# Keys projected first in differential attention, and a first layer whose loads and products come in another order

## The chip, the cores and the metric

The kernel runs on one core of one Trainium2 chip. The metric is the device time of one execution in microseconds. The kernel before takes 3145.52 us, the median of three runs (3144.89 to 3149.38). The profiled execution took 3149.2 us.

The engines are called PE (TensorE, matrix products), DVE (VectorE), ACT (ScalarE), POOL (GpSimd) and SP (SyncE, which here only issues transfers). SBUF is the on-chip memory that they work from, PSUM the one that PE's products are summed in.

## The reference: what is computed

Two transformer blocks run one after the other on 512 tokens of width 1024, in fp32. The first block has two layers and also carries 256 context tokens; the second has two layers of another kind (a gated convolution, dilated window attention, a gated recurrence), which the change leaves as they are.

Every layer normalizes its input and scales and shifts it by a modulation, which comes from a conditioning vector times a large matrix:

```
def _modulate(x, g, shift, scale):
    return _rms_norm(x, g) * (1 + scale) + shift
```

The first layer ("even") then projects tokens and context with `even_w_in`, and runs window attention and neighbourhood attention. The second ("odd") is differential attention with 8 heads. Each head has two query and two key halves of 64, values of 128, and keys and values from the 512 tokens and the 256 context tokens:

```
    q, k, v = _split_odd(hx @ w_in)
    cq, ck, cv = _split_odd(hc @ w_in)
...
    s = jnp.einsum('bqhmd,bkhmd->bhmqk', q, k).astype(jnp.float32) * d ** -0.5
    p = jax.nn.softmax(s, axis=-1)
    a = (p[:, :, 0] - lam * p[:, :, 1]).astype(v.dtype)
    o = jnp.einsum('bhqk,bkhe->bqhe', a, v)
```

Queries and keys of the tokens (not those of the context) are rotated by their position in a grid (rope). No query of the context is needed in this layer.

## The kernel before, in words

Activations lie in SBUF with the features on the 128 partitions, in 8 slices k, tokens along the free axis. To reach fp32 accuracy every operand is split into a high and a low part, and a product is made of three: `mm3` (L140 to L149) issues for each k high weight times high x (L147), high weight times low x (L148), and low weight times high x (L149). A projection of one chunk of 128 output features is 24 products with 512 columns for the tokens and 24 with 256 columns for the context. Its weight is loaded by `weight` (L132): SP issues the load into `wraw`, ACT casts the high part (L129), DVE subtracts the low part (L130). How many buffers `wraw` has is the first number in `b.weights(...)`.

The program is written as a sequence of operations on tiles, with a number of buffers for each tile name (`BUFS`, and `b.bufs.update`). A framework orders each engine's instructions by priorities and sets the semaphores; each engine then runs its own list in order. A transfer is issued by SP or, for the keys' copies, by POOL, in the order of that engine's list.

**The first layer's start, `start_even`.** SP issues the loads: the tokens hx, blocks `adan` of the modulation's matrix (8 of them are needed here, one per slice k), the small vectors, the weights of the first four chunks, the context hc, then constants (`rest()`). PE forms the mean of the squares of the tokens (L224, `xa<-sqx`) and of the context (`xa<-sqc`). Then for each k: `sums(k)` multiplies the conditioning vectors with block k of the matrix (L623), ACT copies the result (L715), `norm(k)` transposes it (L721), DVE adds it up, and `scaled` makes the normalized, modulated slice k of tokens and context, split in two (`axh`, `axl`, `ach`, `acl`). `project(k)` issues slice k of the projections (L733 to L735), two steps behind (`AHEAD`): before, of four chunks for the tokens and of two for the context. The sums lie in PSUM tiles `xa` and `ca`. The context of the last two chunks follows at the end by `mm3`. The four chunks are a key, a value and two query chunks; their chains end in the K, V and Q of the first attention: rope on DVE and POOL, casts on ACT (L302, L490), subtractions on DVE (L303, L491), transfers on POOL (L492, L493), and transposes of V on PE (L322).

**The odd attention, `layer_odd`.** For each head h and query block qb of 128 queries, `softmax` issues two sets of scores (four products each, `s<-K,Q`, L328 and L329: high and low part of the keys), a maximum on DVE (L862), an exponential on ACT (L864), and combines the two maps to `pr` (L865 to L868). `finish` does for the previous query block six transposes on PE (L876), copies on ACT (L877), and products with V (`o<-pT,V`, L879). In blocks 1, 2 and 3 `project(h + 1, part)` projects one part of the next head into the PSUM tile d, which has one buffer; `take` brings it out through a tile `raw`, which has two.

- Part 0, Q: only tokens. Rope (DVE shuffle L287, product with the cosine L288, POOL product with the sine L289, DVE sum L290), then two passes each on ACT (L302) and DVE (L303).
- Part 1, K: tokens and context. Rope, ACT copy of the context (L825), two ACT casts (L310), two DVE subtractions (L311), and four transfers K to K, issued by POOL (L313), that copy half of the partitions to the other half, so that high and low parts lie as the score products need them.
- Part 2, V: tokens and context, copies (L823, L825), six transposes on PE (L322), copies (L323).

The first head's three parts come from the end of the layer before (`first`), in the tile dd, and their order is the order of a list in the program.

Of the kernel before, what the change touches and what calls it, by code (L numbers as in the profile page):

```python
# [9 lines left out]
F32 = mybir.dt.float32  # L10
# [7 lines left out]
P = 128  # L18
D = 1024
KC = D // P  # L20
# [9 lines left out]


AHEAD = 2
BUFS = { "adan": 5, "xa": 4, "ca": 2, "sqx": 3, "sqc": 3, "nwx": 3, "nwc": 3, "adas": 1, "nw": 6, "nr0": 2, "nt": 2,
# [633 lines left out]
def start_even(b, st, mod, pset, chunks, hp, pp, rest):  # L667


    nc, io = b.nc, b.io  # L670
    raw = b.tile(hp, [P, KC, 2], F32, "craw")
    nc.sync.dma_start(raw, io["ccT"])
    nc.vector.memset(st, 0.0)
    nc.scalar.activation(st[:, :, :2], raw, AF.Silu)
    hx = b.tile(hp, [P, KC, T], F32, "hx")
    hc = b.tile(hp, [P, KC, TC], F32, "hc")

    def load(k):
        w = b.tile(hp, [P, KC, 256], F32, "adan")
        nc.sync.dma_start(w, io["ada_wa"][k])  # L680
        return w

    for i in range(0, KC, 2):
        nc.sync.dma_start(hx[:, i:i + 2], io["xT"][:, i:i + 2])
    aw = [load(0)]
    nc.sync.dma_start(b.vecs, io["vecs"])
    ws = [b.weight(io["even_w_in"][chunks[0]])]
    for i in range(0, KC, 4):
        nc.sync.dma_start(hc[:, i:i + 4], io["ctxT"][:, i:i + 4])
    ws.append(b.weight(io["even_w_in"][chunks[1]]))  # L690
    aw.append(load(1))
    ws += [b.weight(io["even_w_in"][ch]) for ch in chunks[2:]]
    aw += [load(k) for k in range(2, 5)]
    rest()
    gm = b.tile(hp, [P, KC], F32, "gm")
    nc.vector.tensor_scalar(gm, b.vec("norm1_g0"), -0.5, None, op0=ALU.mult)
    r = {}

    def rms(key, h, n):
        ms = b.mean(pp, b.squares(hp, n, lambda k: h[:, k], sq="sq" + key), n, tag="xa")  # L700
        r[key] = b.newton(hp, ms, n, key)

    rms("x", hx, T)
    ps = [{"x": b.tile(pp, [P, T], F32, "xa")} for _ in chunks]
    for p in ps[:2]:
        p["c"] = b.tile(pp, [P, TC], F32, "ca")
    parts = pset.all()
    mm = nc.tensor.matmul

    def sums(k):  # L710
        w = aw[k] if k < len(aw) else load(k)
        po = b.tile(pp, [P, 256], F32, "o")
        ada_mm(b, po, st, w)
        sb = b.tile(hp, [P, 256], F32, "adas")
        nc.scalar.copy(sb, po)  # L715
        return sb

    def norm(k, sb):
        pt = b.tile(pp, [P, T], F32, "t")
        for c in range(2):  # L720
            nc.tensor.transpose(pt[:, c * P:(c + 1) * P], sb[:, c * P:(c + 1) * P], b.ident)  # L721
        ada_sum(b, mod, k, 2, pt[:, :256])
        sc = b.tile(hp, [P, 2], F32, f"sc{k}")
        nc.vector.tensor_scalar(sc, mod[:, 8 + k], 1.0, gm[:, k:k + 1], op0=ALU.add, op1=ALU.mult)
        for v, (key, h) in enumerate((("x", hx), ("c", hc))):
            hi, lo = parts[key][k]
            b.scaled(hp, h[:, k], r[key], sc[:, v:v + 1], mod[:, k, v:v + 1], hi, lo, "nw" + key)

    def project(k):
        for (wh, wl), p in zip(ws, ps):  # L730
            for key in p:
                hi, lo = parts[key][k]
                mm(p[key], wh[:, k], hi, start=k == 0, stop=False)  # L733
                mm(p[key], wh[:, k], lo, start=False, stop=False)
                mm(p[key], wl[:, k], hi, start=False, stop=k == KC - 1)  # L735

    for k in range(KC + AHEAD):
        if k < KC:
            sb = sums(k)
        if k == 0:  # L740
            rms("c", hc, TC)
        if k >= AHEAD:
            project(k - AHEAD)
        if k < KC:
            norm(k, sb)
    for w, p in zip(ws[2:], ps[2:]):
        p["c"] = b.tile(pp, [P, TC], F32, "ca")
        b.mm3(p["c"], w, parts["c"])
    return parts, ps


def layer_even(b):
# [7 lines left out]
    with ExitStack() as ps0:  # L760
        pp = b.pool(ps0, "ps0", space=PSUM)
        with ExitStack() as s:
            b.weights(s, "w0", 2, 4)
            a, ps = start_even(b, st, mod, S0, first, b.pool(s, "h0"), pp, A.load)
        A.kp, A.pp = b.pool(att, "kp0"), pp
        for ch, p in zip(first, ps):
            A.take(ch, p)
# [31 lines left out]

def layer_odd(b, a, first, env):
    tc, nc, io = b.tc, b.nc, b.io
    side, other = env.ins.side, env.other
# [1 line left out]
    b.weights(wax, "wa1", 2, 2, side)  # L806
    yp = b.pool(yx, "Y1", side)
    at = b.pool(att, "at1", other)
    ws = [b.weight(io["odd_w_in"][8 * part + 1]) for part in range(2)]
    lam = diff_lambda(b, at)  # L810
    mean_v = b.tile(at, [P, P], F32, "mean_v")
    nc.vector.memset(mean_v, 1.0 / P)
# [5 lines left out]
    def take(part, ps, pp, tag):  # L818
        raw = b.tile(at, [P, TA], F32, "raw")
        if part < 2:  # L820
            b.rope(at, raw[:, :T], ps["x"])
        else:
            nc.scalar.copy(raw[:, :T], ps["x"])  # L823
        if part:
            nc.scalar.copy(raw[:, T:], ps["c"])  # L825
        if part == 0:
            q = b.tile(at, [P, 2, T], F32R, "Q1")
            b.qstack(q, raw, T)
            return (q,)
        if part == 1:  # L830
            k1, k2 = (b.tile(at, [P, 2, TA], F32R, t) for t in ("K1", "K2"))
            b.kstack(k1, k2, raw, TA)
            return k1, k2
        v = b.tile(at, [P, 6, P], F32, "V1")
        b.values(pp, v, raw, 6, tag)
        return (v,)

    def project(h, part):
        w = ws.pop(0) if ws else b.weight(io["odd_w_in"][8 * part + h])
        ps = {}  # L840
        for key, n in (("x", T), ("c", TC))[:1 if part == 0 else 2]:
            ps[key] = b.tile(pp, [P, T], F32, "d")[:, :n]
            b.mm3(ps[key], w, a[key])
        return take(part, ps, pp, "t")

    qkv = sum((take(part, ps, env.pp, "dd") for part, ps in enumerate(first)), ())
    env.pdx.close()
    pp = b.pool(ppx, "pp1", space=PSUM)

# [42 lines left out]
    Y = []  # L892
    before = None
    for h in range(8):
        after = ()
        po = b.tile(pp, [P, T], F32, "o")
        for qb in range(4):
            pr = softmax(qkv, qb)
            if before:
                finish(*before)  # L900
                if qb == 0:
                    Y.append(value(h - 1, before[1]))
            if qb and h < 7:
                after += project(h + 1, qb - 1)
            before = qkv[3], po, qb, pr
        qkv = after
    finish(*before)
    Y.append(value(7, po))

# [667 lines left out]
def program(tc, io):  # L1577
    with ExitStack() as left:
# [20 lines left out]
        nx, gx1 = b.modulation(modx, "norm1_g1", 0)  # L1599
        nc1, _ = b.modulation(modc, "norm1_g1", 0)  # L1600
        w = io["odd_w_in"]
        a, first = next_layer(b, env, rest, {"x": nx, "c": nc1}, streams, [(w[0], "x"), (w[8], "xc"), (w[16], "xc")])
        ops, slots = layer_odd(b, a, first, env)
        n2, g2 = b.modulation(modx, "norm2_g1", 1)
        mod = b.tile(b.cp, [P, 48], F32, "mod2_0")
# [69 lines left out]
```

## Time and profile before

| | |
|---|---|
| median of three runs | 3145.52 us |
| profiled execution | 3149.2 us |
| its span, first to last instruction | 3147.1 us |
| mean granted clock of PE | 0.989 of full speed |
| busy share of PE, DVE, ACT, POOL | 96%, 63%, 42%, 7% |

Times in the rows below are microseconds from the start of the span. A row of a timeline gives start, length, engine, line, operation, what is written and read, how many instructions are merged, and in brackets how long the engine stood idle before and what released it. A row of a stretch gives its length and, for each engine, its busy time and number of instructions, then PE's mean granted clock (1.00 is 2.4 GHz, 0.50 is 1.2 GHz), the share of the transfer engines' time, and GB/s. Products on PE overlap, so their lengths in a timeline add up to more than the time that passes.

### The profile page before, as it was taken

The numbers are of one execution on the slowest core, as the hardware profiler recorded it, in microseconds if no ns is written. First come the engines' busy times: TensorE is split into PE (matmuls) and PEld (weight loads), VectorE is DVE, ScalarE is ACT, GpSimd is POOL, SyncE is SP. The second block draws the span as 40 slices with busy tenths as digits, with TensorE's granted clock in tenths as the row PEclk, the third lists the DMA queues.
The fourth block names the chain that finished last, engine by engine and source line by source line (L and its number), as shares of the span: only waits on it lengthen the run. The fifth ranks groups of instructions, "written<-read, shape, count | busy, mean of one in ns | idle before, by whom it ended". The sixth has DMA issues, their size and how long they took to land.

```text
span 3147.1 us, 48350 instructions
## 1 busy us (share of the span) xinstructions
PE 3026.1 (96%) x19416; PEld 2484.1 (79%) x19416; DVE 1990.6 (63%) x3564; ACT 1310.1 (42%) x2290; POOL 217.7 (7%) x293
## 2 busy tenths in 40 slices
PE   7999999999998999899999999999999999999998
PEld 5776798888897877798888776698888777688887
DVE  6656475545436766676665885677865785674545
ACT  4656441222234555543223354652424354652422
POOL 0000100000011111000002111100001111100000
PEclk9999999999999999999999999999999999999999
DMA  6222423444312122246661232346662132323331
GB/s 241 91 88 91 141 81 121 128 122 127 120 34 66 45 60 54 92 139 189 189 192 41 75 88 82 121 126 190 193 186 76 55 88 81 121 88 95 100 89 52
DMA packets 100336, 342.78 MB, mean 109 GB/s; under 512 B 12176, under 2 KB 15888, under 8 KB 97040
## 3 DMA queue, kind: packets, MB, share of 16 engines
q1 hardware_dynamic: 93840, 325.53, 33.5%
q0 software_dynamic: 5120, 11.01, 1.8%
q8 instruction: 153, 2.51, 0.3%
q10 hardware_dynamic: 1152, 3.15, 0.3%
q14 instruction: 71, 0.58, 0.1%
HBM read 326.54 MB, written 2.10 MB: 104 GB/s over the span
## 4 chain that ended last, share of the span: by engine, by line
PE 80%; DVE 12%; ACT 3%; DMA 2%; issue 2%; POOL 1%; DVEq 0%; SPq 0%; POOLq 0%; ACTq 0%
PE dd L147 18%; PE dd L148 18%; PE dd L149 18%; PE d L147 3%; PE d L148 3%; PE d L149 3%; DMA K<-K 2%; PE o L597 1%; PE s L328 1%; DVE cy L1021 1%; DVE wlo L130 1%; PE s L329 1%; PE t L590 1%; PE o L1097 1%; ACT whi L129 1%
## 5 line engine op out<-in xcount | busy, mean ns | idle before, releaser
L147 PE MATMUL dd<-axh,whi 128*128 128x512 f32 (+1 forms) x2696 | 966.1, 360 | 6.1 <-ACT axh L243 5.9
L148 PE MATMUL dd<-axl,whi 128*128 128x512 f32 (+1 forms) x2696 | 967.0, 360 | 0.6 <-DVE axl L130 0.3
L149 PE MATMUL dd<-axh,wlo 128*128 128x512 f32 (+1 forms) x2696 | 964.7, 359 | 0.0
L129 ACT CAST whi<-wraw 128x1024 fp32r<-128x1024 f32 (+1 forms) x388 | 403.1, 1043 | 1027.1 <-PE dd L148 749.8
L130 DVE TENSOR_TENSOR wlo<-wraw,whi 128x1024 fp32r<-128x1024 f32 (+1 forms) x388 | 468.7, 1212 | 339.5 <-ACT whi L129 321.0
L147 PEld LDWEIGHTS dd<-axh,whi 128*128 128x128 f32 x2696 | 507.2, 189 | 85.1 <-ACT axh L243 7.9
L148 PEld LDWEIGHTS dd<-axl,whi 128*128 128x128 f32 x2696 | 508.3, 189 | 79.2 <-DVE axl L130 1.7
L149 PEld LDWEIGHTS dd<-axh,wlo 128*128 128x128 f32 x2696 | 508.1, 189 | 78.1
L181 DVE CUSTOM_DVE_ANT_0 adaj<-wraw,cond,vecs 128x1024 bf16<-128x1024 f32 x160 | 205.5, 1284 | 145.8 <-DMA wraw<-in_ada_w 87.8
L147 PE MATMUL d<-axh,whi 128*128 128x512 f32 x664 | 276.0, 416 | 6.6 <-ACT axh L129 4.7
L149 PE MATMUL d<-axh,wlo 128*128 128x512 f32 x664 | 272.3, 410 | 1.1 <-DVE wlo L130 1.1
L148 PE MATMUL d<-axl,whi 128*128 128x512 f32 x664 | 269.0, 405 | 0.7 <-DVE axl L130 0.7
L218 POOL TENSOR_TENSOR sq<-sq,sq 128x256 f32<-128x256 f32 x90 | 77.4, 871 | 1989.1 <-ACT sq L213 1871.1
L154 DVE SCALAR_TENSOR_TENSOR hx<-dd,mod,hx 128x512 f32<-128x512 f32 (+1 forms) x109 | 72.0, 661 | 173.8 <-PE dd L149 173.7
L148 PE MATMUL dd<-acl,whi 128*128 128x256 f32 x568 | 160.5, 283 | 0.0
L149 PE MATMUL dd<-ach,wlo 128*128 128x256 f32 x568 | 160.3, 282 | 0.0
L147 PE MATMUL dd<-ach,whi 128*128 128x256 f32 x568 | 160.2, 282 | 0.0
L147 PEld LDWEIGHTS d<-axh,whi 128*128 128x128 f32 x664 | 126.1, 190 | 37.0 <-ACT axh L129 6.1
L149 PEld LDWEIGHTS d<-axh,wlo 128*128 128x128 f32 x664 | 126.0, 190 | 32.1 <-issue 6.3
L148 PEld LDWEIGHTS d<-axl,whi 128*128 128x128 f32 x664 | 126.4, 190 | 27.7 <-issue 4.0
L328 PE MATMUL s<-K,Q 128*128 128x256 f32 (+1 forms) x336 | 116.1, 356 | 30.1 <-DMA K<-K 19.3
L329 PE MATMUL s<-K,Q 128*128 128x512 f32 (+1 forms) x336 | 108.8, 339 | 1.9 <-DMA K<-K 1.9
(384 smaller groups left out, 4470.4 us busy)
## 6 DMA issues: line engine op xcount, KB each, us to landing
wraw<-in_mlp_w SPq DMA_DIRECT2D x128, 512.0 KB, 3.6
wraw<-in_w_ada SPq DMA_DIRECT2D x96, 512.0 KB, 4.0
wraw<-in_w_up SPq DMA_DIRECT2D x88, 512.0 KB, 3.6
wraw<-in_w_in SPq DMA_DIRECT2D x56, 512.0 KB, 3.6
wraw<-in_ada_w SPq DMA_DIRECT2D x48, 512.0 KB, 3.6
adaw<-in_ada_wb SPq DMA_DIRECT2D x16, 1024.0 KB, 4.9
wraw<-in_w_down SPq DMA_DIRECT2D x32, 512.0 KB, 3.5
wraw<-in_odd_w_in SPq DMA_DIRECT2D x24, 512.0 KB, 3.7
```

What stands on the lines that cost most here:

```text
L129: self.nc.scalar.copy(hi, src)
L130: (e or self.nc.vector).tensor_tensor(lo, src, f32(hi), op=ALU.subtract)
L147: mm(ps, hi[:, k], xh[:, sl], start=first, stop=False)
L148: mm(ps, hi[:, k], xl[:, sl], start=False, stop=False)
L149: mm(ps, lo[:, k], xh[:, sl], start=False, stop=last)
L154: self.nc.vector.scalar_tensor_tensor(h, ps, gate[:, m:m + 1], h, op0=ALU.mult, op1=ALU.add)
L181: nc.vector.tensor_tensor_reduce(junk, raw, c, 1.0, self.vec(bias)[:, i:i + 1], ALU.mult, ALU.add, out[:, i:i + 1])
L218: e.tensor_tensor(acc, acc, s2, op=ALU.add)
L328: mm(ps, q[:, slot, toks], k1[:, keys], start=True, stop=False)
L329: mm(ps, q[:, slot, toks], k2[:, keys], start=False, stop=mask is None)
L590: last = nc.tensor.transpose(pt[:, o:o + P], pr[hd][:, i * P:(i + 1) * P], b.ident)
L597: mm = nc.tensor.matmul(po[64 * o:64 * o + 64], v, sbs[i][:, 2 * P * o:2 * P * (o + 1)], start=i == 0, stop=i == len(vts) - 1)
```

## The change

In the odd attention the three parts of the next head come in the order K, Q, V, set by `ORDER = (1, 0, 2)`, where they came as Q, K, V; the first head's parts and the weights loaded ahead follow the same order.

In `start_even` the loads are issued in another order: the second modulation block and the second weight now come before the context, and the constants (`rest()`) are issued at step 7. `wraw` has three buffers there, where it had two. In the loop only three chunks' tokens are projected (there were four); the context's mean is formed at step `LATE` = 2 (was 0), the context is scaled two steps behind the tokens and projected two steps further behind. The fourth chunk's tokens follow by `mm3` after the loop, then the context of the third and fourth. A PSUM tile `ca` has 512 columns and holds the context sums of two chunks: the first and third share one, the second and fourth the other.

The number of instructions is the same on every engine.

```diff
@@ start_even
-    aw = [load(0)]
+    aw, ws = [load(0)], []
     nc.sync.dma_start(b.vecs, io["vecs"])
-    ws = [b.weight(io["even_w_in"][chunks[0]])]
+    project = lambda i: ws.append(b.weight(io["even_w_in"][chunks[i]]))
+    more = lambda: aw.append(load(len(aw)))
+    project(0)
+    more()
+    project(1)
     for i in range(0, KC, 4):
         nc.sync.dma_start(hc[:, i:i + 4], io["ctxT"][:, i:i + 4])
-    ws.append(b.weight(io["even_w_in"][chunks[1]]))
-    aw.append(load(1))
-    ws += [b.weight(io["even_w_in"][ch]) for ch in chunks[2:]]
-    aw += [load(k) for k in range(2, 5)]
-    rest()
+    more()
+    project(2)
+    more()
+    more()
+    project(3)
...
-    ps = [{"x": b.tile(pp, [P, T], F32, "xa")} for _ in chunks]
-    for p in ps[:2]:
-        p["c"] = b.tile(pp, [P, TC], F32, "ca")
+    pc = [b.tile(pp, [P, T], F32, "ca") for _ in chunks[::2]]
+    ps = [{"x": b.tile(pp, [P, T], F32, "xa"), "c": pc[i % 2][:, i // 2 * TC:(i // 2 + 1) * TC]} for i in range(len(chunks))]
...
+        if k == KC - 1:
+            rest()
...
-        for v, (key, h) in enumerate((("x", hx), ("c", hc))):
-            hi, lo = parts[key][k]
-            b.scaled(hp, h[:, k], r[key], sc[:, v:v + 1], mod[:, k, v:v + 1], hi, lo, "nw" + key)
+        scs.append(sc)
+        scaled(k, 0, "x", hx)
+    def scaled(k, v, key, h):
+        hi, lo = parts[key][k]
+        b.scaled(hp, h[:, k], r[key], scs[k][:, v:v + 1], mod[:, k, v:v + 1], hi, lo, "nw" + key)
+    def project(k, key, n):
+        hi, lo = parts[key][k]
+        for (wh, wl), p in zip(ws[:n], ps):
...
     for k in range(KC + AHEAD):
         if k < KC:
             sb = sums(k)
-        if k == 0:
+        if k == LATE:
             rms("c", hc, TC)
         if k >= AHEAD:
-            project(k - AHEAD)
+            project(k - AHEAD, "x", 3)
+        if k >= AHEAD + LATE:
+            project(k - AHEAD - LATE, "c", 2)
         if k < KC:
             norm(k, sb)
+        if k >= LATE:
+            scaled(k - LATE, 1, "c", hc)
+    for k in range(KC + AHEAD - LATE, KC):
+        scaled(k, 1, "c", hc)
+    for k in range(KC - LATE, KC):
+        project(k, "c", 2)
+    b.mm3(ps[3]["x"], ws[3], parts["x"])
     for w, p in zip(ws[2:], ps[2:]):
-        p["c"] = b.tile(pp, [P, TC], F32, "ca")
         b.mm3(p["c"], w, parts["c"])
@@ layer_even
-            b.weights(s, "w0", 2, 4)
+            b.weights(s, "w0", 3, 4)
@@ layer_odd
+ORDER = (1, 0, 2)
-    ws = [b.weight(io["odd_w_in"][8 * part + 1]) for part in range(2)]
+    ws = [b.weight(io["odd_w_in"][8 * part + 1]) for part in ORDER[:2]]
...
-    qkv = sum((take(part, ps, env.pp, "dd") for part, ps in enumerate(first)), ())
+    join = lambda parts: parts[1] + parts[0] + parts[2]
+    qkv = join([take(part, ps, env.pp, "dd") for part, ps in zip(ORDER, first)])
...
-                after += project(h + 1, qb - 1)
+                after.append(project(h + 1, ORDER[qb - 1]))
...
-        qkv = after
+        qkv = join(after) if after else ()
@@ the program
-        a, first = next_layer(b, env, rest, {"x": nx, "c": nc1}, streams, [(w[0], "x"), (w[8], "xc"), (w[16], "xc")])
+        a, first = next_layer(b, env, rest, {"x": nx, "c": nc1}, streams, [(w[8], "xc"), (w[0], "x"), (w[16], "xc")])
```

How the change moves instructions is shown at two places. The first is PE at the end of a head (the one before the boundary at 1107.25 us of the trace). d is the projection of V, its tokens' last product first and its context's first and last; s are the next head's scores, t the transposes of V. Before:

```order
L149 MATMUL d_10633<-axh_1795_9015,wlo_10630 128x512
L328 MATMUL s_10703<-K_2101_10573,Q_2081_10461 128x512
L328 MATMUL s_10712<-K_2101_10573,Q_2081_10461 128x512
L147 MATMUL d_10658<-ach_1765_8985,whi_10629 128x256
...
L149 MATMUL d_10658<-ach_1779_8999,wlo_10630 128x256
L322 MATMUL t_10687<-ident_58,raw_10683 128x128 x4
L329 MATMUL s_10703<-K_2102_10574,Q_2081_10461 128x512
```

The same place on PE now:

```order
L150 MATMUL d_10631<-axh_1793_9013,wlo_10628 128x512
L329 MATMUL s_10701<-K_2080_10485,Q_2100_10576 128x512
L330 MATMUL s_10701<-K_2081_10486,Q_2100_10576 128x512
L329 MATMUL s_10701<-K_2080_10485,Q_2100_10576 128x256
L330 MATMUL s_10701<-K_2081_10486,Q_2100_10576 128x256
L148 MATMUL d_10656<-ach_1763_8983,whi_10627 128x256
...
L150 MATMUL d_10656<-ach_1777_8997,wlo_10628 128x256
L323 MATMUL t_10685<-ident_58,raw_10681 128x128 x4
L329 MATMUL s_10710<-K_2080_10485,Q_2100_10576 128x512
```

The first scores stand at the same place in both, behind the tokens' products of V; before, the first product of each set stood there, now the whole first set. On POOL, for the same head and the beginning of the next, before (rsh is the rotated half in rope, first Q's, then the keys'):

```order
L289 TENSOR_TENSOR rsh_10456<-rsh_10456,sin_132 128x512
L289 TENSOR_TENSOR rsh_10567<-rsh_10567,sin_132 128x512
L313 DMA K_2101_10573<-K_2101_10573 64x768 x2
L313 DMA K_2102_10574<-K_2102_10574 64x768 x2
L289 TENSOR_TENSOR rsh_10831<-rsh_10831,sin_132 128x512
```

And now (first the keys', then, behind their four transfers, Q's):

```order
L290 TENSOR_TENSOR rsh_10479<-rsh_10479,sin_477 128x512
L314 DMA K_2080_10485<-K_2080_10485 64x768
L314 DMA K_2081_10486<-K_2081_10486 64x768
L314 DMA K_2080_10485<-K_2080_10485 64x768
L314 DMA K_2081_10486<-K_2081_10486 64x768
L290 TENSOR_TENSOR rsh_10571<-rsh_10571,sin_477 128x512
```

The keys' product and transfers moved ahead of Q's product. The second place is the start of the program. SP's list before, from the small vectors on:

```order
L686 DMA vecs_66<-in_vecs 128x691
L135 DMA wraw_97<-in_even_w_in 128x1024
L689 DMA hc_89<-in_ctxT 128x1024 x2
L135 DMA wraw_105<-in_even_w_in 128x1024
L680 DMA adan_111<-in_ada_wa 128x2048
L135 DMA wraw_113<-in_even_w_in 128x1024
L135 DMA wraw_119<-in_even_w_in 128x1024
L680 DMA adan_125<-in_ada_wa 128x2048
```

And now:

```order
L687 DMA vecs_66<-in_vecs 128x691
L136 DMA wraw_97<-in_even_w_in 128x1024
L681 DMA adan_103<-in_ada_wa 128x2048
L136 DMA wraw_105<-in_even_w_in 128x1024
L694 DMA hc_89<-in_ctxT 128x1024 x2
L681 DMA adan_113<-in_ada_wa 128x2048
L136 DMA wraw_115<-in_even_w_in 128x1024
L681 DMA adan_121<-in_ada_wa 128x2048
```

The second block of the modulation (adan) and the second weight went ahead of the context, and the third block ahead of the third weight. PE's list at the start before (xa from sqx and sqc are the two means, o the modulation's sums, t their transposes, xa from axh the first projection):

```order
L224 MATMUL xa_173<-sqx_150,mean_d_64 128x512
L623 MATMUL o_219<-adan_94,cst_70 32x256 x8
L721 MATMUL t_261<-ident_58,adas_228 128x128 x2
L623 MATMUL o_276<-adan_111,cst_70 32x256 x5
L224 MATMUL xa_253<-sqc_230,mean_d_64 128x256
L623 MATMUL o_276<-adan_111,cst_70 32x256 x3
L733 MATMUL xa_181<-axh_60_187,whi_99 128x512
```

And now:

```order
L225 MATMUL xa_156<-sqx_133,mean_d_64 128x512
L624 MATMUL o_202<-adan_94,cst_70 32x256 x8
L727 MATMUL t_213<-ident_58,adas_211 128x128 x2
L624 MATMUL o_224<-adan_103,cst_70 32x256 x8
L727 MATMUL t_235<-ident_58,adas_233 128x128 x2
L624 MATMUL o_246<-adan_113,cst_70 32x256 x8
L225 MATMUL xa_280<-sqc_257,mean_d_64 128x256
L741 MATMUL xa_166<-axh_52_170,whi_99 128x512
```

The context's mean still stands ahead of the first projection; a pair of transposes and the third block's sums now do so too.

## Rows read from the trace of the kernel before

**Rows 1.** The page, busy time, share and instructions of each engine.
```profile
PE 3026.1 (96%) x19416; PEld 2484.1 (79%) x19416; DVE 1990.6 (63%) x3564; ACT 1310.1 (42%) x2290; POOL 217.7 (7%) x293
```

**Rows 2.** Waits of PE, 940 to 1330: total us, times, longest.
```profile
PE s L328 <- DMA K<-K: 19.3, 8, 3.3
...
PE t L876 <- DVE pr L868: 2.3, 6, 0.4
...
PE s L329 <- DMA K<-K: 1.9, 1, 1.9
```

**Rows 3.** Stretches of the odd attention: length, busy (count), clock, DMA.
```profile
1060.76:1104.52 43.76, 40.29 (x232) 34.15 (x232) 28.61 (x51) 23.03 (x42) 5.01 (x6) 0.96 0.23 56
...
1148.02:1189.75 41.73, 38.81 (x232) 32.67 (x232) 28.61 (x51) 23.02 (x42) 5.01 (x6) 1.00 0.23 56
...
1275.44:1312.00 36.56, 33.05 (x197) 27.68 (x197) 21.98 (x42) 20.29 (x40) 0.00 (x0) 0.95 0.25 76
```

**Rows 4.** Timeline of PE at a boundary between heads.
```profile
1107.25 0.47 PE L328 MATMUL s<-K,Q 128*128 128x512 f32 x1 [2.74 <-DMA K<-K]
```

**Rows 5.** Chain of waits at the same boundary: start, us, what.
```profile
1101.10 6.02 DMA K<-K
```

**Rows 6.** Timeline of DVE and POOL: the chain of Q.
```profile
1124.35 0.74 DVE L287 STREAM_SHUFFLE rsh<-d 128x512 f32<-128x512 f32 x1
...
1125.24 1.61 POOL L289 TENSOR_TENSOR rsh<-rsh,sin 128x512 f32<-128x512 f32 x1 [21.34 <-DVE rsh L287]
...
1129.82 1.39 DVE L303 SCALAR_TENSOR_TENSOR Q<-raw,Q 64x512 fp32r<-64x512 f32 x2
```

**Rows 7.** Stretches: V's x-products; two score sets and o.
```profile
1098.56:1104.13 5.57, 5.57 (x28) 4.59 (x26) 4.46 (x5) 2.21 (x3) 2.11 (x4) 1.00 0.45 103
1124.28:1127.10 2.82, 2.82 (x24) 2.64 (x22) 2.75 (x7) 1.73 (x4) 1.61 (x1) 1.00 0.00 0
```

**Rows 8.** Timeline of PE, ACT and POOL: the first head.
```profile
974.71 1.54 PE L322 MATMUL dd<-ident,raw 128*128 128x128 f32 x6 [6.87 <-ACT raw L823]
...
984.20 0.47 PE L328 MATMUL s<-K,Q 128*128 128x512 f32 x1 [3.29 <-DMA K<-K]
...
991.89 0.50 PE L328 MATMUL s<-K,Q 128*128 128x512 f32 x1 [2.07 <-ACT pr L864]
...
970.86 1.28 ACT L302 ACTIVATE Q<-raw 64x512 fp32r<-64x512 f32 x2 [5.49 <-DVE raw L290]
...
976.62 1.69 ACT L310 CAST K<-raw 64x768 fp32r<-64x768 f32 x2
...
980.08 0.51 POOL L313 DMA_DIRECT2D K<-K  x1 [0.45 <-DVE lam L933]
```

**Rows 9.** Timeline of PE and of SP's queue at the start.
```profile
20.86 1.89 PE L623 MATMUL o<-adan,cst 128*32 128x256 f32 x10 [3.45 <-DMA adan<-in_ada_wa]
24.57 1.22 PE L224 MATMUL xa<-sqc,mean_d 128*128 128x256 f32 x2 [1.83 <-DVE sqc L218]
...
26.73 0.80 PE L733 MATMUL xa<-axh,whi 128*128 128x512 f32 x1
...
31.37 1.07 PE L623 MATMUL o<-adan,cst 128*32 128x256 f32 x16
...
18.09 4.39 SPq L135 DMA_DIRECT2D wraw<-in_even_w_in  x2
```

**Rows 10.** Stretches of the start, columns as in rows 3.
```profile
0.00:27.00 27.00, 8.60 (x39) 2.86 (x40) 16.25 (x33) 17.85 (x29) 0.21 (x4) 0.86 0.84 320
27.00:72.00 45.00, 44.68 (x306) 34.52 (x306) 28.98 (x63) 16.14 (x33) 5.07 (x5) 0.97 0.60 219
```

**Rows 11.** Waits of PE, 0 to 85.
```profile
PE s L328 <- DVE Q L303: 2.6, 1, 2.6
```

**Rows 12.** Timeline of ACT and POOL: first keys' context sums, last key issue.
```profile
63.18 0.37 ACT L477 COPY raw<-ca 128x256 f32<-128x256 f32 x1 [2.00 <-PE ca L735]
...
72.60 0.51 POOL L493 DMA_DIRECT2D K<-K  x1 [1.40 <-DVE K L491]
```

More of the change, by code (lines that the diff above doesn't have):

```diff
@@ L32 @@
 AHEAD = 2
+LATE = 2
 BUFS = { "adan": 5, "xa": 4, "ca": 2, "sqx": 3, "sqc": 3, "nwx": 3, "nwc": 3, "adas": 1, "nw": 6, "nr0": 2, "nt": 2,
@@ L724, in norm @@
         nc.vector.tensor_scalar(sc, mod[:, 8 + k], 1.0, gm[:, k:k + 1], op0=ALU.add, op1=ALU.mult)
-        for v, (key, h) in enumerate((("x", hx), ("c", hc))):
-            hi, lo = parts[key][k]
-            b.scaled(hp, h[:, k], r[key], sc[:, v:v + 1], mod[:, k, v:v + 1], hi, lo, "nw" + key)
[L729 to L735, printed above, removed]
+        scs.append(sc)
[6 more added lines that the diff above has]
+        for (wh, wl), p in zip(ws[:n], ps):
+            mm(p[key], wh[:, k], hi, start=k == 0, stop=False)
+            mm(p[key], wh[:, k], lo, start=False, stop=False)
+            mm(p[key], wl[:, k], hi, start=False, stop=k == KC - 1)
+    scs = []
     for k in range(KC + AHEAD):
@@ L894, in layer_odd @@
     for h in range(8):
-        after = ()
+        after = []
         po = b.tile(pp, [P, T], F32, "o")
```

## The prediction

> **What bounds the kernel now.** I read the page first, then the waits of TensorE (PE), then stretches of the odd attention and of the start side by side, and at last single instructions around the waits. PE is busy 96% of the span [rows 1], so what only relieves another engine counts for nothing; to be won are PE's idle time and its stretches at the lower clock. The change touches two places.
>
> In the odd attention PE waits 19.3 + 1.9 us for a transfer from K to K [rows 2]: the copies that complete a head's stacked keys. Of this 3.29 us belong to the first head [rows 8]; the other 17.9 us are seven waits at the seven boundaries between heads. One of them: the piece that decides is issued at 1101.10 and under way for 6.02 us [rows 5], and the scores begin at 1107.25 after 2.74 us of idleness [rows 4]. After the keys' projection PE only had the 24 x-products of V to do, 5.57 us [rows 7], and little else. The waits cost a second time: the stretches 1060.76 to 1104.52 and 1148.02 to 1189.75 hold the same 232 products, at a mean granted clock of 0.96 and 1.00, and PE is busy for 40.29 and 38.81 us [rows 3]. That is 1.48 us for a boundary after which PE falls to the lower level (1.2 GHz); four of the seven did, the last among them (0.95, [rows 3]).
>
> At the start PE does the first modulation block, is idle until the second one's weights land at 20.86, waits 1.83 us for the context's squares, and begins the first projection at 26.73 [rows 9]. From 27 to 72 us it is busy for 44.68 of 45.00 [rows 10]. Then a wait of 2.6 us for Q stands before the first scores [rows 11].
>
> **The change, part by part.** No instruction comes or goes, so the sum is one of waits and of the clock. It is made against the profiled execution, 3149.2 us (span 3147.1, and 2.1 around it), which lies 3.7 above the median of 3145.5.
>
> *Heads 1 to 7, keys first.* The keys of the next head are now projected in its predecessor's query block 1, one block earlier, so their casts and transfers have the projections of Q and of V and the scores of a block beside them; a transfer of 6.02 us is over long before. On POOL the keys' four issues now stand ahead of the multiplication for Q's rotation, which comes a block later, so nothing queues behind them. Gain: 17.9 of waits and 4 x 1.48 = 5.9 of clock, together 23.8 us.
>
> What is late next is Q, projected in block 2. Its chain runs in the trace from DVE's shuffle at 1124.35 over POOL's 1.61 to DVE's last pass, 1129.82 + 1.39 = 1131.21: 6.9 us [rows 6]. Its cover after the change: two sets of scores and twelve o products, 2.82, and V's 24 x-products, 5.57, together 8.4 us [rows 7], and six transposes that I don't count. That leaves 1.5 us, so Q ought to be ready, but only just.
>
> Against this stand small new waits. The scratch d has one buffer, so V's first product waits until DVE has read Q's sums out of it; Q's first waits for ACT's copy of the keys' context sums, which may stand behind a weight cast; and o's products in the block after the keys wait for ACT's pT copy, which may stand behind two key casts of together 1.69 [rows 8]. The trace has waits of this kind: six of at most 0.4 us for pr [rows 2]. I take two or three more per head, 1.0 us together; the bounds are none and 2.4 (the two of 0.4 and the casts' 1.69). Over seven heads: +7 (0 to 17).
>
> *The first head.* Before, Q goes first: ACT's first pass on Q starts at 970.86, that on the keys at 976.62, the keys' last issue at 980.08, the first scores at 984.20 after 3.29 us of waiting, and then PE waits 2.07 more for the first exponentials [rows 8]. The keys now take Q's place, 5.8 us earlier, so their last issue comes near 974.3. Q's multiplication on POOL stands behind it; from there Q's chain takes 6.0 us (1125.24 to 1131.21, [rows 6]), to about 980.3. So the scores can start some 3.5 us sooner, and the x-products that stood ahead of them now fill the wait for the exponentials. The 6.87 us before V's transposes [rows 8] stay, since V's copy still needs a raw slot that the other two hold. I take the 3.29 and the 2.07 as gone and 0.6 of clock with them: -6. Bounds: -2 if Q comes as late as the keys did and only the second wait is filled, -9 if the 6.87 shrink too.
>
> *The start.* SyncE's queue now brings the second modulation block and the second weight ahead of the context. The wait up to 20.86 shrinks, but the first projection now stands behind the context's mean in PE's order, and the context lands behind 1.5 MB more: at the 320 GB/s of [rows 10] 4.9 us, at the rate of a full DMA share (320 / 0.84 = 381) 4.1. Its squares were held up by busy engines as well as by its landing, so I take the mean 3.2 later, at 27.8 instead of 24.57 [rows 9]; with its own 1.22 the first projection starts at 29.0, which is 2.3 later. By then PE has done the third block's sums, worth 1.07 in the loop [rows 9], and a pair of transposes more than before. Net about +1. From there on PE has the same number of products and no idle time to lose: fewer projections per step leave each step shorter, but DVE, the busiest beside PE, is at work for only 28.98 of the 45 us [rows 10]. SyncE's stop for a free raw buffer until 18.09 [rows 9] goes, worth nothing, since PE had other work when those weights landed. The 2.6 of [rows 11] stay: Q's raw slot still comes free with V's transposes, which stand behind the last projection. Bounds: -2 (the context no later, the 1.83 gone) and +4 (the mean 4.9 later, or a wait in the loop).
>
> Sum: -23.8 + 7 - 6 + 1 = -21.8, so 3127.4 for the profiled execution and **3124 us** for the median.
>
> **A rule weighed.** The change puts the context sums of two chunks side by side in one PSUM tile of 512 columns. In the trace ACT takes the keys' context sums out at 63.18 and the keys' last issue is at 72.60 [rows 12]. The Trainium skill, "PSUM — Partial Sum Buffer", section "PSUM bank collisions raise a hardware error", says that no two engines may be at one bank in the same partitions at once, disjoint columns or not, so that it is to be guarded by bank and not by address. No row here shows what such a guard would order; what it would cost is the third rival.
>
> **Rivals.**
> 1. *The wait changes its owner.* The small waits come near their upper bound, or Q's chain is 2.5 us longer among the moved work and the scores wait for it by about 1. With 2.4 us per head given back, 17, and 2 at the start: -23.8 + 17 - 6 + 2 = -10.8, **3135**. For it: Q's margin is 1.5 us, and DVE and ACT get the same work in another order. Against it: DVE is busy 63% and ACT 42% [rows 1], and the waits seen are short.
> 2. *Two large waits per head, slower.* If V's first product waits for DVE to read Q out of d, and o's for pT behind the key casts, each as long as the old boundary (2.5), and each also drops the clock (1.48), a place costs 4.0 us. Seven heads with two make 56 against the 29.8 saved with the first head: +26 and the start's +1, **3172**. It decides from a little over one such place per head. Against it: each needs over 2 us of work queued ahead on DVE or ACT, and the short waits of [rows 2] lie in the stretch of clock 1.00 too [rows 3].
> 3. *The keys' context sums copied late at the start.* If the keys' copy waits until the third chunk's sums beside them are done, which is two chunks of context products after 63.18, about 5 us, the keys' last issue moves from 72.60 to 77.7, and with a transfer of 2 to 6 us the scores start at 80 to 84, not at 77.5: +2.5 to +6, **3128**. For it: keys and third chunk share the tile. Against it: the copy has nothing but one weight cast ahead of it on ACT, and the third chunk's sums begin only after the fourth chunk's 24 x-products. By the Trainium skill's page named above the tile would be guarded as one; that is this rival.
> 4. *The boundary stays.* The keys were only the last of several chains, and Q or V takes the old wait over with its clock: 4.0 per head, 28 given back: -23.8 + 28 - 6 + 1 = -0.8, **3145**. For it: V and Q keep ACT and DVE busy there too. Against it: V is needed only by o, a block later, and Q's 6.9 us are shorter than its cover.
>
> **How the numbers follow.** Forecast 0.60 (own range 3115 to 3132), rival 1 0.17, rival 2 0.06, rival 3 0.05, rival 4 0.12. A measurement of this kernel can tell about 0.2% from no change, 6.3 us: faster is below 3139.2. Faster: 0.60 + 0.05 + 0.15 of rival 1 = 0.80; same 0.12 + 0.02 = 0.14; slower 0.06. The range goes from 3111 (no small waits, -9 in the first head, -2 at the start) to 3140 (rival 1 with the start's +4 and more of Q); rivals 2 and 4 are left out.
>
> **What would show it.** Right: the waits of s for K's transfer are gone from PE's list, heads take 39 to 41 us at clock 1.00, the first scores come before 981, and the start's last projection ends within 2 us of before. Wrong: in each head a wait of over 1 us of s for Q, of d for DVE or of o for pT; heads still at 0.96; or a start longer by over 4 us. A gain well past 30 us would mean that stretches behind the attention changed too, whose order of instructions is the same.

## The result, and the profile after

The changed kernel takes 3115.86 us (median of 4 runs, 3114.47 to 3117.41), beside 3147.45 for the kernel before in the same comparison. The ratio is 0.9895 with a 95% interval of 0.9876 to 0.9915. The forecast was 3124, 21.5 us below the median of before; measured are 31.6 less. The range given with the forecast was 3115 to 3132, so the time lies within 1 us of its lower end. The profiled executions took 3149.2 and 3114.5 us, 34.7 apart.

Where the 34.7 us are is read from stretches that begin and end at the same instruction: the whole odd attention from its first wait to the wait behind it, and in it the first head up to the second head's first scores. Heads are counted from 0 where they have a number, as in the prediction: heads 1 to 7 are the second to the last. Columns as in [rows 3]; before:

```profile
967.84:1312.97 345.13, 310.11 (x1778) 259.92 (x1778) 231.04 (x418) 184.99 (x332) 39.78 (x48) 0.96 0.24 59
...
967.84:1019.32 51.48, 38.63 (x188) 31.65 (x189) 35.18 (x68) 21.88 (x40) 10.09 (x12) 0.87 0.31 71
```

The same two stretches after, and one later head, which answers to the first line of [rows 3]:

```profile
968.60:1278.59 309.99, 299.35 (x1779) 251.79 (x1778) 236.47 (x418) 186.79 (x334) 38.06 (x48) 0.99 0.25 66
...
968.60:1012.49 43.89, 35.00 (x189) 28.64 (x189) 35.53 (x68) 22.55 (x41) 10.14 (x12) 0.92 0.34 79
...
1051.50:1090.46 38.96, 38.69 (x233) 32.83 (x232) 29.58 (x51) 23.30 (x41) 4.65 (x6) 1.00 0.23 61
```

The attention is 35.1 us shorter. Of that, 24.4 are idle time of PE (345.13 - 310.11 = 35.0 before, 309.99 - 299.35 = 10.6 after), and 10.8 are busy time for the same products, which is for the most part the clock. The first head gives 7.6, the seven boundaries and what follows them 27.5 (345.13 - 51.48 = 293.65 before, 309.99 - 43.89 = 266.10 after). In front of the attention 0.8 us were lost (967.84 against 968.60), behind it nothing changed: 1834.1 and 1833.8 us from there to the end of the span. A later head now takes 39.0 us at clock 1.00, with 0.3 us of idleness, where it took 41.4 to 43.8.

PE's waits from 940 to 1330 after, total, times and longest, answer to [rows 2]:

```profile
PE dd L323 <- ACT raw L846: 7.6, 1, 7.6
PE d L148 <- ACT axh L130: 4.3, 1, 4.3
PE o L903 <- ACT pT L901: 1.1, 6, 0.2
PE s L329 <- issue: 0.8, 1, 0.8
PE s L329 <- ACT pr L888: 0.4, 1, 0.4
```

No wait for K is left, and the six waits of 0.4 for pr are gone too. What is left of more than 1 us in one piece is the wait for V's copy in the first head (it was 6.9) and one behind the attention (it was 4.6).

Q's chain after, in the timeline of DVE and POOL, against [rows 6]:

```profile
1081.55 0.74 DVE L288 STREAM_SHUFFLE rsh<-d 128x512 f32<-128x512 f32 x1
...
1082.45 1.27 POOL L290 TENSOR_TENSOR rsh<-rsh,sin 128x512 f32<-128x512 f32 x1 [4.66 <-DVE rsh L288]
...
1085.40 1.40 DVE L304 SCALAR_TENSOR_TENSOR Q<-raw,Q 64x512 fp32r<-64x512 f32 x2
```

It takes 5.3 us, not 6.9, and Q is ready at 1086.8, 3.7 us ahead of the scores at 1090.46 (the end of the stretch above). In the old order DVE did other work between the passes, so that the sum came 3.8 us after the shuffle (1128.18); now it comes 2.2 us after it (1083.75).

The start after, in PE's timeline, against [rows 9] and [rows 11]:

```profile
23.47 1.41 PE L624 MATMUL o<-adan,cst 128*32 128x256 f32 x16 [3.84 <-DMA adan<-in_ada_wa]
27.20 1.22 PE L225 MATMUL xa<-sqc,mean_d 128*128 128x256 f32 x2 [2.32 <-DVE sqc L219]
27.86 0.99 PE L741 MATMUL xa<-axh,whi 128*128 128x512 f32 x1
...
77.72 0.58 PE L329 MATMUL s<-K,Q 128*128 128x256 f32 x1 [2.80 <-DVE Q L304]
```

The wait for the second block became one of 3.84 for the third, the mean of the context came 2.6 us later, and the first scores came 0.2 later (77.72, where 77.5 was before).

### The profile page after: what moved, and what is told of

The parts are those of the page before. It is cut to its first block, busy times and chain, and to the rows that moved or that the text cites. A ratio compares the mean times of both kernels' runs of the same rounds, so it can differ in the third digit from the quotient of the medians.

```text
span 3112.4 us, 48373 instructions
## 1 busy us (share of the span) xinstructions
PE 3012.5 (97%) x19416; PEld 2475.7 (80%) x19416; DVE 1993.3 (64%) x3564; ACT 1311.9 (42%) x2290; POOL 216.3 (7%) x293
## 4 chain that ended last, share of the span: by engine, by line
PE 85%; DVE 9%; ACT 3%; issue 1%; DMA 1%; POOL 1%; DVEq 0%; SPq 0%; POOLq 0%; ACTq 0%
PE dd L148 18%; PE dd L149 18%; PE dd L150 18%; PE d L148 4%; PE d L149 4%; PE d L150 4%; PE s L329 2%; PE s L330 2%; PE o L903 2%; PE o L598 2%; DVE cy L1045 1%; PE o L1121 1%; PE t L591 1%; DVE wlo L131 1%; DVE qs L1173 1%
## 5 line engine op out<-in xcount | busy, mean ns | idle before, releaser
L150 PE MATMUL dd<-axh,wlo 128*128 128x512 f32 (+1 forms) x2696 | 965.0, 359 | 0.0
L150 PEld LDWEIGHTS dd<-axh,wlo 128*128 128x128 f32 x2696 | 508.1, 189 | 78.1
L150 PE MATMUL d<-axh,wlo 128*128 128x512 f32 x664 | 272.4, 410 | 1.1 <-DVE wlo L131 1.1
L150 PE MATMUL dd<-ach,wlo 128*128 128x256 f32 x568 | 160.4, 282 | 0.0
L150 PEld LDWEIGHTS d<-axh,wlo 128*128 128x128 f32 x664 | 125.4, 189 | 31.7 <-issue 6.3
L149 PEld LDWEIGHTS d<-axl,whi 128*128 128x128 f32 x664 | 125.5, 189 | 27.8 <-issue 3.8
L329 PE MATMUL s<-K,Q 128*128 128x512 f32 (+1 forms) x336 | 115.5, 355 | 10.2 <-DVE st L1100 3.9
L148 PEld LDWEIGHTS dd<-ach,whi 128*128 128x128 f32 x568 | 107.9, 190 | 2.5
```

Of the source, the lines that this page charges most:

```text
L148: mm(ps, hi[:, k], xh[:, sl], start=first, stop=False)
L149: mm(ps, hi[:, k], xl[:, sl], start=False, stop=False)
L150: mm(ps, lo[:, k], xh[:, sl], start=False, stop=last)
L329: mm(ps, q[:, slot, toks], k1[:, keys], start=True, stop=False)
```

## The experiments

All ratios are to the kernel before on the same chip, with their 95% intervals; the changed kernel's is 0.9895.

**1 and 2, the parts apart.** One kernel has only the odd attention's edits, the other only those of `start_even` and its buffers.

> Only the odd attention's part of the change (keys first, in the first head too); the first layer's start is that of before. Theory: the whole gain is in the odd attention, where the changed kernel's trace is 35.1 us shorter, and the start costs 0.7; so 34 to 36 us below before, ratio about 0.989, and no transfer of K in PE's waits. Rival: the start's new order gives back or brings several us that show only later, so this kernel gains less than 30 or more than 40.

> Only the first layer's part; the odd attention is that of before. Theory: no change that can be told, +0.7 us (0 to +2), the seven waits for K as before. Rival: the earlier loads are worth 3 us or more, then it is faster by over 0.1%.

Measured: odd attention alone 3115.86 us, 0.9893 (0.9878 to 0.9908), which is 33.7 us less than before by the ratio and 35.4 by the medians; start alone 3153.23 against 3151.28, 1.0006 (0.9997 to 1.0015). The whole gain is the odd attention's. Both theories held, and the start's rival (3 us or more) is out.

**3, the first head in the old order.** The edit is shown against experiment 1.

```diff
-    qkv = join([take(part, ps, env.pp, "dd") for part, ps in zip(ORDER, first)])
+    qkv = sum((take(part, ps, env.pp, "dd") for part, ps in enumerate(first)), ())
-    ... [(w[8], "xc"), (w[0], "x"), (w[16], "xc")])
+    ... [(w[0], "x"), (w[8], "xc"), (w[16], "xc")])
```

> Start of before; keys first for heads 1 to 7, but the first head's three parts come in the old order Q, K, V. Theory: the seven boundaries alone are worth 27.6 us and the first head 7.6, so 26 to 29 below before, and the first head keeps its wait of about 3.3 us for the transfer of K. Rival: the first head's share comes from the later heads' order (its filling products), then this gains 33 or more.

Measured: 3123.80 us, 0.9917 (0.9903 to 0.9930), by the medians 27.5 less than before and 7.9 more than experiment 1. Its one wait for K is the first head's, in PE's waits:

```profile
PE s L328 <- DMA K<-K: 3.9, 1, 3.9
```

So the first head's order is worth its 7.6 us by itself.

**4, Q last.** Heads 1 to 7 project K, V, Q.

```diff
-ORDER = (1, 0, 2)
+ORDER = (1, 2, 0)
-    join = lambda parts: parts[1] + parts[0] + parts[2]
+    join = lambda parts: parts[2] + parts[0] + parts[1]
...
```

> The changed kernel with the order K, V, Q for heads 1 to 7 (first head unchanged), so that Q is projected last. Theory: a wait is the exposed chain less its cover. Q's chain took 5.3 us from the last product to the last Q in the changed kernel (6.9 before), and behind Q's products PE's list holds six transposes, twelve o products and nine products of the next projection, about 3.9 us: so the scores wait for Q 1.3 to 3 us at each boundary, some of the waits drop the clock (1.5 each), and it is 10 to 30 us slower than the changed kernel. Rival: only the transfer of K matters, Q's chain is hidden anywhere: within 3 us of the changed kernel.

Measured: 3144.42 us, 0.9981 (0.9973 to 0.9990), by the ratios 27 us slower than the changed kernel. The size was in the range, the mechanism was not. PE's waits of its heads 1 to 6 (1012 to 1275):

```profile
PE o L904 <- ACT pT L902: 5.2, 7, 0.7
PE s L329 <- ACT pr L889: 3.4, 6, 0.6
PE d L148 <- DVE raw L289: 3.1, 6, 0.5
PE s L329 <- DVE Q L304: 1.5, 6, 0.2
```

and one of its heads as a stretch:

```profile
1064.16:1106.24 42.08, 39.77 (x233) 32.89 (x233) 29.60 (x52) 23.03 (x42) 4.92 (x6) 1.00 0.23 56
```

The scores wait only 0.2 us for Q, so that the time fell into the range is luck. A head takes 3.1 us more than in the changed kernel, in small waits on ACT and DVE (2.3 idle against 0.3) and 1.1 of PE's own time, at full clock; what the 1.1 are is not shown. The last head has two longer waits for pr, 1.2 and 2.1 us. These waits are of the kind and size that the prediction feared, for its tiles d and pT, though not at its places: the products with d wait for DVE to read the keys' own tokens out of it (L289), and o waits for pT in the block of Q, where the copy stands behind a weight cast (ACT, 1100.73 and 1101.69) and not behind the keys' casts. In the order K, V, Q they exist, in K, Q, V not.

**5, useless work in the wait.** The kernel before, with 12 products that nobody reads.

```diff
             b.mm3(ps[key], w, a[key])
+            if part == 2 and key == "x":
+                pt = b.tile(pp, [P, T], F32, "t")
+                for i in range(12):
+                    nc.tensor.matmul(pt, w[0][:, 0], a["x"][0][0], start=True, stop=True)
```

> The kernel before with 12 useless products of 512 columns added in each head, behind V's products with the tokens and into a scratch tile; with them PE's list has the next head's scores behind V's context products too. Theory: a wait for K costs twice, once itself and once by the clock that falls after it. The useless work is 7 x 12 x 0.23 = 19 us, the waits that it covers 17.9 us; the clock stays at 1.00 in every head from the second on, so it is 4 to 8 us faster than before although PE does more. Rival: the lower clock has nothing to do with the waits: it stays at 0.96 in several heads, and the kernel is 0 to 3 us slower.

Measured: 3145.06 us, 0.9972 (0.9962 to 0.9982), 8 to 9 us faster than before with more work. One head, and then heads 1 to 7 together, all at full clock:

```profile
1042.14:1083.82 41.68, 41.23 (x245) 34.99 (x244) 29.04 (x52) 23.03 (x42) 4.67 (x6) 1.00 0.24 58
...
1018.43:1304.59 286.16, 282.76 (x1675) 238.45 (x1673) 197.61 (x350) 163.01 (x292) 27.96 (x36) 1.00 0.23 58
```

That a wait costs twice, itself and the clock behind it, is shown: with the waits covered, partly by the useless products and partly because V's context products now stand ahead of the scores too, no head from the second on is below 1.00. Heads 1 to 7 took 293.65 us before, with 22.2 idle; here they take 286.16 with 3.4 idle. PE is busy for 11.3 us more, though the useless products alone take about 19 (84 of some 0.23 us): the other 8 us are what the clock gave back.

**6 and 9, another issuer for the transfers.** The kernel before, order Q, K, V; SP issues the keys' copies in one, ACT in the other (`nc.scalar`). The edit in short form (the engine is handed in as an argument):

```diff
-                nc.gpsimd.dma_start(K[64 - a:128 - a, i, :n], K[a:a + 64, i, :n])
+                nc.sync.dma_start(f32(K[64 - a:128 - a, i, :n]), f32(K[a:a + 64, i, :n]))
```

> The kernel before, order Q, K, V, with the four transfers K to K of each head of the odd attention issued by SP instead of POOL. Theory: the wait is the time of the transfer that POOL issues (2.6 to 6.2 us from issue to landing in the trace of before); SP's loads of half a megabyte land in about 3.7, so the wait at each boundary shrinks by 1 to 2.5 us, and it is 8 to 20 us faster than before. Rival: the wait is set by the casts and subtractions ahead of the issue, or the transfers stand behind a weight load that waits for its buffer on SP: no faster than before.

Measured: 3121.76 us, 0.9899 (0.9885 to 0.9912), 31 us less: far more than expected, nearly the whole gain of the change, with the old order. The time from issue to landing of the keys' copies (minimum, median, maximum) was, over heads 2 to 7 of the kernel before:

```profile
DMA to landing us min/median/max: 2.6/5.3/6.2
```

and with SP as issuer:

```profile
DMA to landing us min/median/max: 2.5/2.6/2.6
```

One difference is the issuer, another what runs beside. In SP's queue the next weight load now stands behind the four copies; with POOL as issuer SP sent it off among them (1101.27 in the timeline of before, between POOL's issues at 1101.10 and 1102.63). SP's queue in this experiment at one boundary:

```profile
1088.37 3.61 SPq L313 DMA_DIRECT2D K<-K  x4
1092.08 7.00 SPq L135 DMA_DIRECT2D wraw<-in_odd_w_in  x2
```

Experiment 9 tells the two apart, since with ACT as issuer SP is free to load beside the copies again.

> The kernel before, order Q, K, V, with the four transfers K to K of each head issued by ACT, so that SP still issues the next weight load while they are under way. With SP as issuer the transfers took 2.5 to 2.6 us each and the weight load came behind them; with POOL those that ran beside the weight load took 5.3 to 6.0, the one ahead of it 2.6. Theory: the wait was made by the weight load beside the transfers, not by POOL's path: those that run beside it take 4 us or more here too, and waits for K remain. Rival: POOL's path is slow; then all take under 3 us and the waits are gone.

Measured: 3139.42 us, 0.9963 (0.9950 to 0.9976). Landing over the same heads, and PE's waits:

```profile
DMA to landing us min/median/max: 2.5/2.9/5.6
```

```profile
PE s L329 <- DMA K<-K: 11.6, 7, 2.5
...
PE s L328 <- DMA K<-K: 3.0, 1, 3.0
```

The second line is the first head's. By the single transfers of its trace, those issued behind a weight load took 4.0 to 5.6 us, those ahead of one 2.5 to 2.7. At the one boundary whose four copies (issued 1051.91 to 1054.84) had no weight load beside them, all took 2.5 to 3.2 and PE did not wait. With no load beside them POOL's copies are as short: in the changed kernel the first two of each of heads 2 to 7 landed in 2.5 to 2.6. So the load of half a megabyte makes the copies long.

The issuer has a share all the same: ACT's copies that were issued 0.45 us ahead of a load took 2.7, POOL's that were issued 0.17 us ahead of one took 5.6 to 6.2 in the kernel before (the copy that decided, at 1101.10, is one of them), and in the changed kernel those issued 0.8 us ahead still took 3.6 to 5.4. About 12 of the 31 us came with ACT as issuer already, the rest with SP, whose load stands behind the copies. Why a load reaches copies that POOL issued ahead of it is not shown.

**7, a third raw buffer** in the changed kernel's odd attention (`"raw": 3`).

> The changed kernel with three raw buffers in the odd attention, where it has two. Theory: the 7.6 us before the first head's transposes of V wait for a raw slot that the keys hold; with a third slot they go, but the next head's products then wait for their split weight (about 975) and the scores still for Q (about 980), so it wins 1 to 3 us. Rival: Q's chain comes earlier too because ACT and DVE get another order, then 5 us or more.

Measured: 3116.46 us, 0.9886 (0.9872 to 0.9901): no change that can be told. The wait in question only shrank from 7.6 to 6.4, and the scores waited 1.6 us for pr where it was 0.4:

```profile
PE dd L323 <- ACT raw L846: 6.4, 1, 6.4
```

and the attention took 311.0 us, 1.0 more than in the changed kernel. The theory that the slot was all that held V's copy fell. ACT's timeline in the changed kernel shows what does:

```profile
971.68 1.68 ACT L311 CAST K<-raw 64x768 fp32r<-64x768 f32 x2 [2.67 <-DVE raw L291]
973.38 1.99 ACT L130 CAST whi<-wraw 128x1024 fp32r<-128x1024 f32 x2
975.59 0.59 ACT L846 COPY raw<-dd 128x512 f32<-128x512 f32 x1 [0.21 <-DVE K L312]
```

ACT is at work on the keys' casts and two weight casts up to 975.37 and waits for the slot only 0.21 us more; with the third slot V's copy came at 974.02, still behind the keys' casts and one weight cast.

**8, 11 and 10, a later context, and both cures at once.** `LATE = 3`, `LATE = 4`, and `LATE = 3` with the keys' copies by SP, all in the changed kernel.

> The changed kernel with LATE = 3: the context's mean, scaling and products come one step later still. Theory: what holds the first projection in the changed kernel is the context's mean in front of it, which waits until 27.2 us; now twelve products of the first two chunks stand ahead of the third modulation block, in the 3.8 us in which PE waits for that block, and the start ends 2 to 4 us earlier. Rival: PE then waits for the context or for the third chunk's weight later in the loop, and nothing is won.

> The changed kernel with LATE = 4, the context four steps late. Theory: with LATE = 3 nothing before the first projections waits for the context any more, so another step wins nothing: within 2 us of that kernel. Rival: the context's mean still stands in the way in the loop, then 2 to 4 us faster.

> The changed kernel with LATE = 3 and with the odd attention's keys copied by SP. Theory: keys first and keys by SP remove the same wait, so the second adds nothing to the first: within 2 us of the changed kernel with LATE = 3 alone (0.9875 of before). Rival: they remove different parts, and this is 5 us or more faster than that.

Measured: 3114.36 us, 0.9875 (0.9862 to 0.9889); 3111.73 us, 0.9879 (0.9863 to 0.9895); 3114.18 us, 0.9878 (0.9859 to 0.9897). Keys by SP add nothing to keys first, as the theory had it: both remove the same wait. The start did become shorter in the traces, with three steps by 1.1 us where 2 to 4 were expected. With three steps the first projections fill the wait for the third block (PE's timeline):

```profile
21.61 1.22 PE L741 MATMUL xa<-axh,whi 128*128 128x512 f32 x2 [0.88 <-ACT axh L244]
...
27.82 1.28 PE L624 MATMUL o<-adan,cst 128*32 128x256 f32 x16
...
76.63 0.58 PE L329 MATMUL s<-K,Q 128*128 128x256 f32 x1 [2.70 <-DVE Q L304]
```

The first scores came at 76.63 with three steps and at 74.33 with four, against 77.72. The further 2.3 us of four steps, which I had not expected, can't be put down to the step; what it is worth stays open. One of the first projections takes 0.40 us there and 0.63 with three, which are the lengths of the full and of the lower clock elsewhere in these traces (the granted clock that the profile states from 17 to 28 us is 1.00 for both). And the two traces part before the step can act, at the first block's transposes, up to which PE's lists are the same (three steps above, four below):

```profile
16.94 0.69 PE L727 MATMUL t<-ident,adas 128*128 128x128 f32 x2 [0.49 <-ACT adas L721]
...
17.03 0.44 PE L727 MATMUL t<-ident,adas 128*128 128x128 f32 x2 [0.49 <-ACT adas L721]
```

In the total the three versions are not told apart from one another, and from the changed kernel by 1 to 2 tenths of a per cent at most, within their intervals.

## Why the prediction was right, and where its terms were off

Sign, place and mechanism held: the seven waits for K went, their clock came back, Q's chain was covered, the start was worth nothing. The gain was undersized by 13 us in the profile, and the time is only just in the range.

- *Waits for K, -17.9.* Held: none is left, and experiments 5 and 6 remove those at the boundaries by two other ways.
- *Clock, -5.9 for heads 1 to 7.* Measured 7.1 (310.11 - 38.63 = 271.48 us of busy PE in them before, 299.35 - 35.00 = 264.35 after): the last head had lost 1.87 to the lower clock, three others 1.5 to 1.6, and the heads without a drop give 0.6 together.
- *Small new waits, +7.* This term was mis-sized, by far the most: measured -2.5. Idle time of PE from the second head's first scores on went from 22.2 (293.65 less 271.48 busy) to 1.8 us (266.10 less 264.35), 20.4 less, 17.9 of it for K. The old waits for pr went as well, and none of the feared ones came at a size that counts: between Q's products and V's, PE's list has scores and transposes, so d is free when V needs it, and o waits at most 0.2 us for pT. Experiment 4 shows waits for d and pT of 0.5 and 0.7 us in another order, where PE has less ahead of them. I had looked for what could queue on ACT and DVE, and not gone through what PE itself has ahead of each wait. The upper bound, 2.4 a head, was added up wrongly as well (two of 0.4 and 1.69 are 2.5); nothing hangs on it.
- *Q's margin, 1.5 us.* It was 3.7, since the chain took 5.3 and its cover, with the transposes that were not counted, 8.9 (1081.55 to 1090.46).
- *First head, -6.* Measured -7.6, otherwise made up than worked out: 4.0 of idle time (3.29 became 0.85, 2.07 became 0.41, but 6.87 became 7.63; the rest in smaller waits) and 3.6 of clock where 0.6 was taken. The scores came at 980.33, forecast was about 980.3, but that is luck, as POOL's and PE's timelines show:

```profile
972.50 1.27 POOL L290 TENSOR_TENSOR rsh<-rsh,sin 128x512 f32<-128x512 f32 x1 [1.63 <-DVE rsh L288]
...
975.12 1.53 POOL L314 DMA_DIRECT2D K<-K  x3 [0.84 <-DVE K L312]
...
980.33 0.47 PE L329 MATMUL s<-K,Q 128*128 128x512 f32 x1 [0.85 <-issue]
```

Q's multiplication stood ahead of the keys' issues here and not behind them, and the last of these came near 976.1, not 974.3; Q was then held up on DVE, whose sum came only at 978.16, behind the keys' subtractions and two of weights. That V's copy is held by its slot was right only in part (experiment 7).

- *Start, +1.* Measured +0.8; the mean at 27.20 was forecast at 27.8.
- *The sign for a gain well past 30 us*, that stretches behind the attention changed too, was wrong: the profiles are 34.7 apart, and behind the attention nothing changed.

Of the rivals, the third came true in its mechanism and cost nothing. The keys' context sums were copied late, by the third chunk's products (L150 is `mm3`; the keys' own sums are L741 to L743). ACT and POOL after, against [rows 12]:

```profile
68.23 0.37 ACT L478 COPY raw<-ca 128x256 f32<-128x256 f32 x1 [11.05 <-PE ca L150]
...
73.48 0.53 POOL L494 DMA_DIRECT2D K<-K  x1
```

The keys' own sums were complete before 59.8, but the copy waited for the third chunk's last product and came at 68.23. So the tile is guarded as one here. The Trainium skill ("PSUM — Partial Sum Buffer", section "PSUM bank collisions raise a hardware error") asks that PSUM be guarded by bank and not by address; the trace agrees, though what would happen without the guard no run shows. Against 63.18 the copy is 5.05 us later, as worked out, but partly by luck: the working took two chunks of context products from 63.18 on, and what stood between were the fourth chunk's products with the tokens and one chunk of context products. The step of the rival that failed is the next one: the keys' last issue moved by 0.9 us, not by 5, because before it had been held up behind the copy anyway: DVE's second subtraction waited 1.74 us, by the profile for PE's context products, in the timeline of before

```profile
71.35 0.95 DVE L491 TENSOR_TENSOR K<-raw,K 64x768 fp32r<-64x768 f32 x1 [1.74 <-PE ca L148]
```

and the scores, which wait for Q, came at 77.72.

Rival 1 (the wait changes its owner), rival 2 and rival 4 are refuted by the waits above: no single wait over 0.2 us is left in the heads from the second on.

## What to carry to other kernels

When the last piece of a chain is a transfer, look at what else is under way at that moment before moving work: here either projecting the keys earlier or letting SP issue four small copies, which put a weight load behind them, removed the same waits, and doing both gained nothing more. Price a wait of PE with the clock behind it; here four of seven waits of 1.9 to 2.9 us were followed by the lower clock, which cost 1.5 to 1.9 us each time (they were not the four longest: 2.35 was, 2.59 was not). And before charging a new order with new small waits, go through the in-order list of the engine that would wait, since what it has ahead of each place decides whether a wait is seen at all.

## What the runs showed of the hardware that I had not expected

In heads 2 to 7 a copy of 192 KB within SBUF took 2.5 to 2.6 us with no load beside it when POOL or SP issued it, and 2.5 to 3.2 by ACT. Issued behind a load of 512 KB it took 4.0 to 5.6 us by ACT and 4.9 to 5.5 by POOL; POOL's copies took 5.6 to 6.2 even when they were issued 0.17 us ahead of the load, ACT's 2.7 at 0.45 us ahead, SP's 2.6 at 0.55 us ahead. Twelve products per head whose result nobody reads made the kernel before 8 to 9 us faster, because with them PE did not stand still at the boundaries and kept its 2.4 GHz (granted clock 1.00 over heads 1 to 7, 0.98 before).
